# Softmax attention by pairs of heads on the two halves of the array, and one pool of split weights at the low end of the partitions

## Chip, cores and metric

The kernel runs on one core of a Trainium2 chip. The metric is device time in microseconds (us) for one launch: one decoder layer over 512 tokens of width 1024.

## The reference

The layer normalises x, multiplies it by one wide matrix `w_in`, and hands column ranges of the product to three branches: gated linear attention (GLA, 4 heads), softmax attention by blocks (MoBA, 8 heads of 64), and a short convolution. With 512 tokens and blocks of 256 the choice of blocks takes all earlier ones, so that MoBA is plain causal attention with a bias that is linear in the distance:

```
h = rmsnorm(x, g_mix_pre);  gq, gk, gv, gr, glr, mq, mk, mv, sb, sc, sx, glog = split(h @ w_in)
br_a = gla(gq, gk, gv, gr, glr)
br_b = softmax(mq @ mk.T / 8 - slope[head] * distance, causal) @ mv      # 8 heads of 64
br_c = sb * conv3(sc * sx)
merged = sum of sigmoid(glog_i) * (br_i @ w_br_i)
x = x + rmsnorm(merged @ w_out, g_mix_post)
u = conv3(rmsnorm(x, g_ffn_pre) @ ffn_w_up) + b
x = x + rmsnorm((silu(u_gate) * u_up) @ ffn_w_down, g_ffn_post)
```

## The kernel before

**Split weights.** Each large product is made of three matmuls in the type fp32r. `split_w` turns a loaded tile `raw` into `whi` (ACT copies it, line 82) and `wlo` (DVE subtracts, line 83); activations have a high and a low part as well (`hh`/`hl`, `h2h`/`h2l`, `mh`/`ml`, `ahi`/`alo`, and `brA`, `brB`, `brC`). `mm3` (line 91) then issues high by high, high by low and low by high. Where the result has channels on the partitions, `cols_cm` and `up_mm` hold the weights still (the stationary operand, 128 columns) and stream the 512 tokens past them. In `row_major`, which does `w_out` and `w_down`, the activations stand still and 512 columns of weights stream.

**Order of the work.** TensorE's (PE's) instructions stand in the order of the code. A `Stream` called `main` yields after each 12 matmuls of a projection ("a batch" below), and `main.beside(side)` puts pieces of GLA or MoBA between the batches. ACT, DVE and GpSimd (POOL) are ordered by a scheduler; loads are issued on SP's queue.

**MoBA before.** For each of 8 heads `scores` makes two fp32r matmuls for each of the row blocks 3, 2, 1 (line 630 with 128 rows, line 631 with 64 rows) and one fp32 matmul for block 0 (line 633), out of the copies `qs`, `ks`, `kl` that ACT and DVE have made (lines 618 to 622). DVE adds the bias and finds the maximum out of PSUM (line 638), ACT takes the exponential (641), DVE normalises (644). `transposed` turns the probabilities (654), and `mixed` multiplies them by `mv`: 4 fp32 matmuls with 64 stationary columns (669). PSUM has 8 banks: 3 with the tag "main", 5 with "side"; all of MoBA uses the latter.

**Where tiles lie.** Each partition's memory is filled from both ends. Pools without `side` stack up from the low end, pools with `side="right"` from the high end. In the built program, in KB from the start of a partition:

| tile | before | after |
|---|---|---|
| `whi`, `wlo` of the mixer, `w_br`, `w_out` | 190 to 224 | 20 to 62 |
| `whi`, `wlo` of the last `w_out` tile, of `w_up`, `w_down` | 36 to 76 | 20 to 62 |
| `hh`, `hl` | 20 to 52 | 62 to 94 |
| `brA`, `brB`, `brC`, high and low parts | 58 to 130 | 94 to 166 |
| `mh`, `ml` (pool "merged") | 141 to 173 | 175 to 207 |
| `h2h`, `h2l` | 84 to 116 | 98 to 130 |
| `ahi`, `alo` | 130 to 150 | 78 to 98 |

**Buffers of split weights.** In the mixer there are 4 each of `whi` and `wlo` and 2 of `raw`. A second pool "weights2" has 5 and 1; the last tile of `w_out` (k = 7) and the first four of `w_up` (`first_up`, called before the last part of `w_out`) go there. `row_major` keeps its last 4 weight tiles until its last matmul.

Of the kernel before, what the change touches and what calls it, by code (L numbers as in the profile page):

```python
# [17 lines left out]
NT = 4  # L18
# [13 lines left out]
def hybrid_layer(ctx: ExitStack, tc: tile.TileContext, x, g_mix_pre, w_in, gla_w_lr2, gla_b_lr,  # L32
# [34 lines left out]
    def load_w(src, shape):  # L67
        raw = wpool[0].tile([P, wpool[2]], F32, tag="raw", name=nm("raw"), bufs=wpool[1])
# [107 lines left out]
    def load_v(u):  # L176
        raw = wpool[0].tile([P, 2176], F32, tag="raw", name=nm("vraw"), bufs=2)
# [39 lines left out]

    gc = pool("mixer_const")
    b8 = pool("b8")
# [13 lines left out]
    def hi_v(u, half):  # L233
        n = 272 if u == 0 else 256
        hi, lo = [wpool[0].tile([P, wpool[3]], F32R, tag=tag, name=nm(tag), bufs=wpool[4])[:, :4 * n].rearrange(
# [63 lines left out]
    for s in (32, 16, 8, 4, 2, 1):  # L299
# [11 lines left out]
    base = gc.tile([P, T], F32, name="base")  # L311
    nc.gpsimd.iota(base, pattern=[[1, T]], base=-384, channel_multiplier=-1,
                   allow_small_or_imprecise_dtypes=True)
    nc.gpsimd.affine_select(base, base, pattern=[[-1, T]], compare_op=OP.is_ge, fill=-1e37,
                            base=384, channel_multiplier=1)
# [100 lines left out]
    cx = pool("sc", side="right")  # L416
# [62 lines left out]
    def gla_pair(ct, across):  # L479
# [20 lines left out]
        for h in range(2):  # L500
            at.append(gp.tile([P, NT, P], F32, tag="at", name=nm("at"), bufs=3))
# [96 lines left out]
    gp.release()  # L598

    main.beside(iter(["moba"]))
    mp = pool("moba", side="right")
    brB = (bigr("brB_hi"), bigr("brB_lo"))
# [3 lines left out]
    def scores(hd):  # L608
        hs = slice(64 * (hd % 2), 64 * (hd % 2) + 64)
        q, k = mq[hs, hd // 2], mk[hs, hd // 2]  # L610
        bias = mp.tile([P, T], F32, tag="bias", name=nm("bias"), bufs=2)
        nc.gpsimd.tensor_scalar(bias, base, 2.0 ** -(hd + 1), None, op0=OP.mult)

        os_ = slice(64 - hs.start, 128 - hs.start)
        qs = mp.tile([P, T], F32R, tag="qs", name=nm("qs"), bufs=2)
        ks = mp.tile([P, T], F32R, tag="ks", name=nm("ks"), bufs=2)
        kl = mp.tile([P, T], F32R, tag="kl", name=nm("kl"), bufs=2)
# [6 lines left out]
        pr, out_ = {}, {}  # L624
        for i in (3, 2, 1, 0):
            n = (i + 1) * P
            out_[i] = banks[i][:, :n] if i else banks[1][:, 256:384]
            c = slice(i * P, (i + 1) * P)
            if i:
                nc.tensor.matmul(out_[i], qs[:, c], ks[:, :n], start=True, stop=False)  # L630
                nc.tensor.matmul(out_[i], qs[hs, c], kl[hs, :n], start=False, stop=True)  # L631
            else:
                nc.tensor.matmul(out_[i], q[:, c], k[:, :n], start=True, stop=True)
        for i in (3, 2, 1, 0):
            n, ps = (i + 1) * P, out_[i]
            s = mp.tile([P, n], F32, tag=f"p{i}", name=nm("p"), bufs=2)
            mx = sp.tile([P, 1], F32, tag="mx", name=nm("mx"))
            nc.vector.tensor_tensor_reduce(out=s, in0=bias[:, T - n:], in1=ps, scale=-1.0,
                                           scalar=3e38, op0=OP.add, op1=OP.min, accum_out=mx)
            sm = sp.tile([P, 1], F32, tag="sm", name=nm("sm"))  # L640
            last_exp[0] = nc.scalar.activation(s, s, AF.Exp, bias=mx, scale=-1.0, accum_out=sm)
            rc = sp.tile([P, 1], F32, tag="rc", name=nm("rc"))
            nc.vector.reciprocal(rc, sm)
            nc.vector.tensor_scalar(s, s, rc, None, op0=OP.mult)
            pr[i] = s
        return pr

    def transposed(pr):
# [6 lines left out]
        for j in range(3):  # L655
            n = (NT - j) * P if j < 2 else 384
            pt = mp.tile([P, T], F32, tag="pt", name=nm("pt"), bufs=4)
            if j % 2:
                nc.vector.tensor_copy(pt[:, :n], banks[j][:, :n])
            else:  # L660
                nc.scalar.activation(pt[:, :n], banks[j][:, :n], AF.Copy)
            pts.append(pt)
        return pts[0], pts[1][:, :384], pts[2][:, :256], pts[2][:, 256:384]

    def mixed(hd, pts):
        hs = slice(64 * (hd % 2), 64 * (hd % 2) + 64)
# [3 lines left out]
        nc.scalar.activation(brB[0][hs, hd // 2], po[hs], AF.Copy)  # L670
        nc.vector.tensor_tensor(brB[1][hs, hd // 2], po[hs], brB[0][hs, hd // 2].bitcast(F32), OP.subtract)

    def moba():
        pr = pts = None
        for step in range(9):
            nxt = scores(step) if step < 8 else None
            yield 3 if step == 0 else 1
            if pr is not None:
                pts = transposed(pr)
                yield 1  # L680
                mixed(step - 1, pts)
                yield 1
            pr = nxt
# [35 lines left out]
    gc.release()  # L719
# [5 lines left out]
    wpB = pool("weights2")  # L725
# [11 lines left out]
    def row_major(w, kk, resident, getl, epilogue, middle=None):  # L737
# [4 lines left out]
        for k in range(0, kk, 2):  # L742
            raw = load_w(w[k * P:(k + 2) * P].rearrange("(k p) c -> p k c", p=P), (2, D))
            for e in range(2):
                kt = k + e
                wpA = list(wpool)
                if kt == kk - 1:
                    wpool[:] = [wpB, 1, 2048, 1024, 5]
                wts.append([z[:, 0] for z in split_w(raw[:, e:e + 1], 1, D)])
                wpool[:] = wpA  # L750
# [21 lines left out]
    def post_norm(pl, acc, g, res, dst):  # L772
# [4 lines left out]
        def square(n):  # L777
            junk = pl.tile([P, 512], F32, tag="sq", name=nm("sq"), bufs=1)
# [18 lines left out]
    def epi1(t, accs, late=False):  # L797
# [6 lines left out]
        post_norm(ep, accs[t], g2, x1[:, t], x1[:, t])  # L804
# [20 lines left out]
    def first_up():  # L825
        wpA, wpool[:] = list(wpool), [wpB, 1, 2048, 1024, 5]
        ws.extend((part, e, w) for part in range(2) for e, w in enumerate(up_unit(0, part)))
        wpool[:] = wpA
# [4 lines left out]
    wpool[0].release()  # L833
    wpool[:] = [wpB, 1, 2048, 1024, 5]

# [38 lines left out]
    def get_a(k):  # L874
        hi = dn.tile([P, T], F32R, tag="ahi", name=nm("ahi"), bufs=5)
# [40 lines left out]
```

## Time and profile before

| | |
|---|---|
| median of 3 runs | 927.41 us (926.38 to 927.90) |
| the profiled execution | 926.64 us, of which its span 924.8 us |
| PE busy (matmul) | 912.4 us, 99% of the span |
| DVE, ACT, POOL busy | 468.4, 352.2, 76.3 us |
| mean granted clock of PE | 0.994 of full speed |

The span runs from the first to the last instruction; 1.84 us of the execution lie around it. Matmuls overlap one another in the profile (each lasts longer than the time until the next one starts), so what one matmul costs is read from the distance of two starts and not from its length. An fp32 matmul is recorded as two instructions, one in fp32r as one.

### The profile page before, as it was taken

To read this page: it belongs to the slowest core of one execution; us is meant where nothing else is said; L and a number is where in the kernel's file an instruction comes from. 1 tells how busy PE (TensorE), PEld (TensorE's weight loads), DVE (VectorE), ACT (ScalarE), POOL (GpSimd) and SP (SyncE) were. 2 spreads that over 40 slices of the span, in tenths; PEclk is the share of its full clock that TensorE was granted. 3 is DMA by queue.
4 is the path that set the end of the run, shared out by engine and by line. 5 is a ranking of instruction groups with operands and counts; after the bars stand their busy time and mean duration, and the time that the engine had idled before them with its cause. 6 is when DMAs were issued, how large, how long until landed. Compare 5 with 4: busy or idle time off the path is not lost.

```text
span 924.8 us, 11510 instructions
## 1 busy us (share of the span) xinstructions
PE 912.4 (99%) x4723; PEld 737.6 (80%) x4723; DVE 468.4 (51%) x743; ACT 352.2 (38%) x531; POOL 76.3 (8%) x87
## 2 busy tenths in 40 slices
PE   8999989999999999999999999999999999999997
PEld 6988778977667788888888889888888888888885
DVE  5724656487776324242424485665555555433324
ACT  4337644255544323222222354443343333332222
POOL 1001321121010002020201010000000000000000
PEclk8999999999999999999999999999999999999999
DMA  8232312212111132423325511332222333222212
GB/s 255 78 104 73 91 47 57 83 48 90 46 45 47 46 114 68 137 69 105 100 90 184 182 46 69 126 102 92 91 91 91 104 112 103 91 91 91 91 45 92
DMA packets 68616, 85.33 MB, mean 92 GB/s; under 512 B 2693, under 2 KB 62291, under 8 KB 68564
## 3 DMA queue, kind: packets, MB, share of 16 engines
q1 hardware_dynamic: 67522, 84.53, 28.4%
q8 instruction: 37, 0.61, 0.3%
q10 hardware_dynamic: 1042, 0.07, 0.1%
q14 instruction: 15, 0.12, 0.0%
HBM read 82.50 MB, written 2.10 MB: 91 GB/s over the span
## 4 chain that ended last, share of the span: by engine, by line
PE 93%; ACT 4%; DVE 2%; issue 1%; POOL 0%; DVEq 0%; POOLq 0%; ACTq 0%
PE ps L91 84%; PE ps L669 2%; PE ps L563 1%; PE ps L631 1%; PE ps L654 1%; PE ps L169 1%; PE ps L630 1%; ACT whi L82 1%; ACT E L515 1%; PE ps L201 1%; ACT E L516 1%; DVE E L514 1%; DVE wlo L83 0%; PE ps L533 0%; DVE ad L542 0%
## 5 line engine op out<-in xcount | busy, mean ns | idle before, releaser
L83 DVE TENSOR_TENSOR wlo<-raw,whi 128x1024 fp32r<-128x1024 f32 x142 | 177.9, 1255 | 211.7 <-ACT whi L82 211.6
L82 ACT ACTIVATE whi<-raw 128x1024 fp32r<-128x1024 f32 x142 | 149.7, 1058 | 243.6 <-PE ps L91 192.2
L91 PE MATMUL ps<-hh,whi 128*128 128x512 f32 x416 | 168.8, 406 | 0.0
L91 PE MATMUL ps<-hl,whi 128*128 128x512 f32 x416 | 164.5, 395 | 0.0
L91 PE MATMUL ps<-hh,wlo 128*128 128x512 f32 x416 | 164.5, 395 | 0.0
L91 PE MATMUL ps<-h2h,whi 128*128 128x512 f32 (+1 forms) x384 | 142.8, 372 | 0.0
L91 PE MATMUL ps<-h2l,whi 128*128 128x512 f32 (+1 forms) x384 | 142.6, 371 | 0.0
L91 PE MATMUL ps<-h2h,wlo 128*128 128x512 f32 (+1 forms) x384 | 142.6, 371 | 0.0
L91 PEld LDWEIGHTS ps<-hh,whi 128*128 128x128 f32 x416 | 78.2, 188 | 20.4 <-issue 1.7
L91 PEld LDWEIGHTS ps<-hh,wlo 128*128 128x128 f32 x416 | 78.2, 188 | 18.9
L91 PEld LDWEIGHTS ps<-hl,whi 128*128 128x128 f32 x416 | 78.3, 188 | 16.9
L91 PEld LDWEIGHTS ps<-h2l,whi 128*128 128x128 f32 x384 | 72.4, 188 | 12.6
L91 PEld LDWEIGHTS ps<-h2h,whi 128*128 128x128 f32 x384 | 72.3, 188 | 12.5
L91 PEld LDWEIGHTS ps<-h2h,wlo 128*128 128x128 f32 x384 | 72.3, 188 | 12.3
L91 PE MATMUL ps<-whi,ahi 128*128 128x512 f32 x176 | 69.6, 396 | 0.0
L91 PE MATMUL ps<-wlo,ahi 128*128 128x512 f32 x176 | 69.6, 396 | 0.0
L91 PE MATMUL ps<-whi,alo 128*128 128x512 f32 x176 | 69.6, 395 | 0.0
L852 DVE SCALAR_TENSOR_TENSOR u<-ps,cw,u 128x511 f32<-128x511 f32 x44 | 32.9, 747 | 41.7 <-ACT u L849 23.7
L714 POOL TENSOR_TENSOR gate<-gate 128x512 f32<-128x512 f32 x16 | 24.0, 1502 | 217.2 <-DVE gate L712 204.2
L91 PEld LDWEIGHTS ps<-whi,alo 128*128 128x128 f32 x176 | 33.1, 188 | 8.0
L91 PEld LDWEIGHTS ps<-wlo,ahi 128*128 128x128 f32 x176 | 33.1, 188 | 8.0
L91 PEld LDWEIGHTS ps<-whi,ahi 128*128 128x128 f32 x176 | 33.1, 188 | 7.9
(210 smaller groups left out, 1217.8 us busy)
## 6 DMA issues: line engine op xcount, KB each, us to landing
raw<-in_w_in_dram SPq DMA_DIRECT2D x28, 1024.0 KB, 5.5
raw<-in_ffn_w_up_dram SPq DMA_DIRECT2D x22, 1024.0 KB, 5.1
raw<-in_ffn_w_down_dram SPq DMA_DIRECT2D x11, 1024.0 KB, 5.1
x<-in_x_dram SPq DMA_DIRECT2D x8, 512.0 KB, 7.1
raw<-in_w_out_dram SPq DMA_DIRECT2D x4, 1024.0 KB
vraw<-in_w_in_dram SPq DMA_DIRECT2D x4, 512.0 KB, 6.6
raw<-in_w_br_gla_dram SPq DMA_DIRECT2D x4, 512.0 KB, 4.7
raw<-in_w_br_moba_dram SPq DMA_DIRECT2D x4, 512.0 KB, 3.9
```

The source lines that it names most:

```text
L82: nc.scalar.activation(hv, src, AF.Copy)
L83: (sub or nc.vector).tensor_tensor(lv, src, hv.bitcast(F32), op=OP.subtract)
L91: last = nc.tensor.matmul(ps, l, r, start=start and i == 0 and j == 0, stop=stop and i == n - 1 and j == 2)
L169: nc.tensor.transpose(ps[:, i * P:(i + 1) * P], h[:, k * P:(k + 1) * P], ident)
L201: nc.tensor.matmul(ps, warm[:, :P], warm, start=True, stop=True)
L514: nc.vector.tensor_tensor(ev, Lv, Lv[:, :, s - 1:s].to_broadcast([P, nb, 2 * s]), OP.subtract)
L515: nc.scalar.activation(e, e, AF.Abs)
L516: nc.scalar.activation(e, e, AF.Exp, scale=-1.0)
L563: nc.tensor.matmul(po[:, c], l, v[:, j, cv], start=j == 0, stop=j == i)
L669: nc.tensor.matmul(po[hs, j * P:], mv[:, j, hd * 64:(hd + 1) * 64], pts[j], start=j == 0, stop=j == NT - 1)
L714: nc.gpsimd.tensor_tensor(g, g, acc, op=OP.add)
L852: nc.vector.scalar_tensor_tensor(u[:, 1:], ps[:, :T - 1], cw[:, 1, j:j + 1], u[:, 1:], op0=OP.mult, op1=OP.add)
```

## The change

Four things change. (1) One pool of split weights with 5 buffers each of `whi` and `wlo` lies at the low end of the partitions for the whole kernel, the pool of raw tiles (2 buffers) at the high end, and "weights2" is gone; `ahi` and `alo` get a pool at the low end. (2) `scores` and `mixed` work on pairs of heads. The scores are plain fp32 matmuls straight from `mq` and `mk`, one head on rows 0 to 63 of the array and the other on rows 64 to 127, in turns, in two groups (row blocks 3 and 2, then 1 and 0) with a batch between; `mixed` has one head on columns 0 to 63 and the other on 64 to 127, in turns, and leaves PSUM for both heads at once. `qs`, `ks` and `kl` are gone. (3) `base`, from which the biases are made, is computed by POOL when MoBA begins and not in the setup. (4) Smaller: GLA's `at` has 2 buffers and not 3; the squares in the last epilogue are written into `o` and not into a tile of their own.

```
-    wpool = [pool("weights", side="right"), 2, 2176, 1088, 4]
+    wp = pool("weights")
+    rw = pool("raw_weights", bufs=2, side="right")
...
-            hi = wpool[0].tile([P, wpool[3]], F32R, tag="whi", name=nm("whi"), bufs=wpool[4])
-            lo = wpool[0].tile([P, wpool[3]], F32R, tag="wlo", name=nm("wlo"), bufs=wpool[4])
+            hi = wp.tile([P, 1088], F32R, tag="whi", name=nm("whi"), bufs=5)
+            lo = wp.tile([P, 1088], F32R, tag="wlo", name=nm("wlo"), bufs=5)
...
-            at.append(gp.tile([P, NT, P], F32, tag="at", name=nm("at"), bufs=3))
+            at.append(gp.tile([P, NT, P], F32, tag="at", name=nm("at"), bufs=2))
...
+    base = mp.tile([P, T], F32, name="base")
+    nc.gpsimd.iota(base, pattern=[[1, T]], base=-384, channel_multiplier=-1,
+                   allow_small_or_imprecise_dtypes=True)
+    nc.gpsimd.affine_select(base, base, pattern=[[-1, T]], compare_op=OP.is_ge, fill=-1e37,
+                            base=384, channel_multiplier=1)
...
-        nc.scalar.activation(qs[hs], q, AF.Copy)
-        nc.scalar.activation(ks[hs], k, AF.Copy)
-        nc.vector.tensor_tensor(qs[os_, P:], q[:, P:], qs[hs, P:].bitcast(F32), OP.subtract)
-        nc.vector.tensor_copy(ks[os_], ks[hs].bitcast(F32))
-        nc.vector.tensor_tensor(kl[hs], k, ks[hs].bitcast(F32), OP.subtract)
-        banks = {3: psum(), 2: psum(), 1: psum()}
...
-                nc.tensor.matmul(out_[i], qs[:, c], ks[:, :n], start=True, stop=False)
-                nc.tensor.matmul(out_[i], qs[hs, c], kl[hs, :n], start=False, stop=True)
...
+        for group in ((3, 2), (1, 0)):
+            out_ = {}
+            for i in group:
+                for e in range(2):
+                    out_[i, e] = psum() if i else out_[1, e][:, 256:384]
+            for i in group:
+                n = (i + 1) * P
+                for e in range(2):
+                    hs = slice(64 * e, 64 * e + 64)
+                    nc.tensor.matmul(out_[i, e][:, :n], mq[hs, pair, i * P:(i + 1) * P], mk[hs, pair, :n],
+                                     start=True, stop=True)
...
-            nc.tensor.matmul(po[hs, j * P:], mv[:, j, hd * 64:(hd + 1) * 64], pts[j], start=j == 0, stop=j == NT - 1)
+            for e in range(2):
+                hd = 2 * pair + e
+                nc.tensor.matmul(po[64 * e:64 * e + 64, j * P:], mv[:, j, hd * 64:(hd + 1) * 64], pts[e][j],
+                                 start=j == 0, stop=j == NT - 1)
...
+        yield from scores(0)
+        yield 2
+        for pair in range(4):
+            if pair < 3:
+                yield from scores(pair + 1)
+            pts = []
+            for e in range(2):
+                pts.append(transposed(ready[pair][e]))
+                yield 1 + e
+            mixed(pair, pts)
+            yield 1
...
-                wpA = list(wpool)
-                if kt == kk - 1:
-                    wpool[:] = [wpB, 1, 2048, 1024, 5]
...
-        hi = dn.tile([P, T], F32R, tag="ahi", name=nm("ahi"), bufs=5)
-        lo = dn.tile([P, T], F32R, tag="alo", name=nm("alo"), bufs=5)
+        hi = ah.tile([P, T], F32R, tag="ahi", name=nm("ahi"))
+        lo = ah.tile([P, T], F32R, tag="alo", name=nm("alo"))
```

On PE, the scores of the second head before (one head, 7 matmuls in one piece):

```order
L630 MATMUL ps_2083<-ks_2076,qs_2075 128x512
L631 MATMUL ps_2083<-kl_2077,qs_2075 128x512
L630 MATMUL ps_2084<-ks_2076,qs_2075 128x384
L631 MATMUL ps_2084<-kl_2077,qs_2075 128x384
L630 MATMUL ps_2085<-ks_2076,qs_2075 128x256
L631 MATMUL ps_2085<-kl_2077,qs_2075 128x256
L633 MATMUL ps_2085<-mk,mq 128x128
```

And of the second pair of heads now, with the first matmuls of the batch behind them (`hh,whi` and so on are that batch's):

```order
L627 MATMUL ps_2123<-mk,mq 128x512
L627 MATMUL ps_2124<-mk,mq 128x512
L627 MATMUL ps_2125<-mk,mq 128x384
L627 MATMUL ps_2126<-mk,mq 128x384
L93 MATMUL ps_2168<-hh,whi_2164 128x512
L93 MATMUL ps_2168<-hl,whi_2164 128x512
```

The second group of the pair (256, 256, 128 and 128 columns) stands 12 matmuls of the batch later. Two heads have 8 fp32 matmuls where they had 12 in fp32r and 2 in fp32, and neighbours belong to different heads.

The product with `mv` on PE, before (one head) and now (a pair):

```order
L669 MATMUL ps_2174<-pt_2150,mv 64x512
L669 MATMUL ps_2174<-pt_2152,mv 64x384
L669 MATMUL ps_2174<-pt_2154,mv 64x256
L669 MATMUL ps_2174<-pt_2154,mv 64x128
L91 MATMUL ps_2161<-hh,whi_2157 128x512
```

```order
L669 MATMUL ps_2323<-pt_2244,mv 64x512
L669 MATMUL ps_2323<-pt_2283,mv 64x512
L669 MATMUL ps_2323<-pt_2246,mv 64x384
L669 MATMUL ps_2323<-pt_2285,mv 64x384
L669 MATMUL ps_2323<-pt_2248,mv 64x256
L669 MATMUL ps_2323<-pt_2287,mv 64x256
L669 MATMUL ps_2323<-pt_2248,mv 64x128
L669 MATMUL ps_2323<-pt_2287,mv 64x128
```

The same matmuls in the same number; those of two heads now alternate.

On ACT, between the last weights of `w_out` and the first epilogue, before (`raw_4313` and `raw_4323` are of `w_out`, `raw_4333` and `raw_4343` of `w_up`'s first unit, `sq` is the first square of the epilogue of token tile 0):

```order
L82 ACTIVATE whi_4319<-raw_4313 128x1024
L82 ACTIVATE whi_4335<-raw_4333 128x1024
L82 ACTIVATE whi_4339<-raw_4333 128x1024
L82 ACTIVATE whi_4325<-raw_4323 128x1024
L82 ACTIVATE whi_4345<-raw_4343 128x1024
L82 ACTIVATE whi_4349<-raw_4343 128x1024
L779 ACTIVATE sq_4379,ss_730_4377<-ps_4189 128x512
L779 ACTIVATE sq_4383,ss_730_4377<-ps_4190 128x512
```

And now (`raw_4236` and `raw_4246` are of `w_up`'s first unit, `raw_4730` of its second; `sq_4451` and `sq_4455` belong to token tile 3, the last):

```order
L778 ACTIVATE sq_4451,ss_736_4449<-ps_4098 128x512
L175 ACTIVATE h2h<-ps_4423 128x4x128
L161 ACTIVATE h_4404,ss_4403<-x_4072 128x1024
L175 ACTIVATE h2h<-ps_4430 128x4x128
L84 ACTIVATE whi_4242<-raw_4236 128x1024
L84 ACTIVATE whi_4248<-raw_4246 128x1024
L84 ACTIVATE whi_4252<-raw_4246 128x1024
L778 ACTIVATE sq_4455,ss_736_4449<-ps_4099 128x512
L175 ACTIVATE h2h<-ps_4497 128x4x128
L175 ACTIVATE h2h<-ps_4504 128x4x128
L84 ACTIVATE whi_4732<-raw_4730 128x1024
L161 ACTIVATE h_4465,ss_4464<-x_4072 128x1024
```

Three of the four splits for `w_up`'s first unit have moved from ahead of the epilogues into the last one; only one of them (of `raw_4236`) still stands ahead.

## Rows read from the trace of the kernel before

**Rows 1.** The page, busy time of each engine (share) xinstructions.
```profile
PE 912.4 (99%) x4723; PEld 737.6 (80%) x4723; DVE 468.4 (51%) x743; ACT 352.2 (38%) x531; POOL 76.3 (8%) x87
```

**Rows 2.** Waits of PE: engine line <- releaser: us in total, times, longest.
```profile
PE ps L563 <- ACT at L545: 2.5, 2, 2.1
```

**Rows 3.** Chain that ended last, in time order: start us, us, what.
```profile
73.08 1.07 PE ps L433 x4
...
131.01 1.38 PE ps L563 x10
```

**Rows 4.** Line 91 on PE, in a stretch of GLA: busy (x), clock, DMA.
```profile
74.00:131.00 57.00, 44.90 (x180) 1.00 0.25 75
```

**Rows 5.** Timeline of PE in four stages: start us, us, engine, line, operands.
```profile
329.77 0.40 PE L91 MATMUL ps<-hh,wlo 128*128 128x512 f32 x1
...
340.04 0.40 PE L91 MATMUL ps<-brA_lo,whi 128*128 128x512 f32 x1
...
514.85 0.39 PE L91 MATMUL ps<-wlo,mh 128*128 128x512 f32 x1
...
521.88 0.39 PE L91 MATMUL ps<-whi,ml 128*128 128x512 f32 x1
...
649.82 0.39 PE L91 MATMUL ps<-h2l,whi 128*128 128x512 f32 x1
...
659.79 0.39 PE L91 MATMUL ps<-h2h,whi 128*128 128x512 f32 x1
...
804.68 0.39 PE L91 MATMUL ps<-whi,alo 128*128 128x512 f32 x1
...
814.95 0.39 PE L91 MATMUL ps<-wlo,ahi 128*128 128x512 f32 x1
```

**Rows 6.** Timeline of PE, one head of MoBA.
```profile
220.89 0.39 PE L630 MATMUL ps<-ks,qs 128*128 128x512 f32 x1
...
223.23 0.50 PE L91 MATMUL ps<-hh,whi 128*128 128x512 f32 x1
...
230.13 2.37 PE L669 MATMUL ps<-pt,mv 128*64 128x512 f32 x8
232.43 0.50 PE L91 MATMUL ps<-hh,whi 128*128 128x512 f32 x1
```

**Rows 7.** Timeline of PE in GLA: matmuls on halves and quarters of the array.
```profile
141.80 0.38 PE L492 MATMUL ps<-QA,KA 64*128 64x256 f32 x1
141.80 0.37 PE L488 MATMUL ps<-QA,KA 64*128 64x128 f32 x1
...
142.23 0.38 PE L493 MATMUL ps<-QA,KA 64*128 64x128 f32 x2
...
168.31 0.22 PE L533 MATMUL ps<-E 64*64 64x64 f32 x1
...
168.37 0.22 PE L533 MATMUL ps<-E 64*64 64x64 f32 x1
```

**Rows 8.** Windows, the stretch of MoBA: PE, PEld, DVE, ACT, POOL busy (x).
```profile
194.00:317.00 123.00, 123.00 (x530) 86.14 (x529) 83.60 (x207) 61.99 (x130) 13.04 (x8) 1.00 0.18 55
```

**Rows 9.** Groups on POOL in the setup: xcount | busy us, mean ns | idle.
```profile
L314 POOL TENSOR_SCALAR_AFFINE_SELECT base<-base 128x512 f32<-128x512 f32 x1 | 0.6, 607 | 0.0
```

**Rows 10.** Timeline around the end of `w_out`.
```profile
552.72 0.28 PE L91 MATMUL ps<-h2h,whi 128*128 128x256 f32 x1
...
557.48 1.06 ACT L159 ACTIVATE h<-x 128x1024 f32<-128x1024 f32 x1 [0.16 <-DVE x L791]
...
559.48 1.29 DVE L161 SCALAR_TENSOR_TENSOR h<-x,rs,g 128x1024 f32<-128x1024 f32 x1 [0.66 <-POOL rs L138]
...
562.22 1.04 PE L169 MATMUL ps<-ident,h 128*128 128x128 f32 x8
```

**Rows 11.** Groups on DVE: xcount | busy us, mean ns | idle, releaser.
```profile
L83 DVE TENSOR_TENSOR wlo<-raw,whi 128x1024 fp32r<-128x1024 f32 x142 | 177.9, 1255 | 211.7 <-ACT whi L82 211.6
```

**Rows 12.** DMA issues: xcount, KB each, median us from issue to landing.
```profile
raw<-in_ffn_w_up_dram SPq DMA_DIRECT2D x22, 1024.0 KB, 5.1
```

More of the change, by code (lines that the diff above doesn't have):

```diff
@@ L67, in load_w @@
     def load_w(src, shape):
-        raw = wpool[0].tile([P, wpool[2]], F32, tag="raw", name=nm("raw"), bufs=wpool[1])
+        raw = rw.tile([P, 2176], F32, tag="raw", name=nm("raw"))
         n = 1
@@ L176, in load_v @@
     def load_v(u):
-        raw = wpool[0].tile([P, 2176], F32, tag="raw", name=nm("vraw"), bufs=2)
+        raw = rw.tile([P, 2176], F32, tag="raw", name=nm("vraw"))
         n = 272 if u == 0 else 256
@@ new lines, in scores @@
+    def scores(pair):
+        bias, pr = [], [{}, {}]
+        for e in range(2):
+            bias.append(mp.tile([P, T], F32, tag="bias", name=nm("bias"), bufs=2))
+            nc.gpsimd.tensor_scalar(bias[e], base, 2.0 ** -(2 * pair + e + 1), None, op0=OP.mult)
+        for group in ((3, 2), (1, 0)):
[9 more added lines that the diff above has]
+                                     start=True, stop=True)
+            for i in group:
+                n = (i + 1) * P
+                for e in range(2):
+                    ps = out_[i, e][:, :n]
+                    s = mp.tile([P, n], F32, tag=f"p{i}", name=nm("p"), bufs=4)
+                    mx = sp.tile([P, 1], F32, tag="mx", name=nm("mx"))
+                    nc.vector.tensor_tensor_reduce(out=s, in0=bias[e][:, T - n:], in1=ps, scale=-1.0,
+                                                   scalar=3e38, op0=OP.add, op1=OP.min, accum_out=mx)
+                    sm = sp.tile([P, 1], F32, tag="sm", name=nm("sm"))
+                    last_exp[0] = nc.scalar.activation(s, s, AF.Exp, bias=mx, scale=-1.0, accum_out=sm)
+                    rc = sp.tile([P, 1], F32, tag="rc", name=nm("rc"))
+                    nc.vector.reciprocal(rc, sm)
+                    nc.vector.tensor_scalar(s, s, rc, None, op0=OP.mult)
+                    pr[e][i] = s
+            yield 1
+        ready.append(pr)
@@ L656, in transposed, with mixed @@
             n = (NT - j) * P if j < 2 else 384
-            pt = mp.tile([P, T], F32, tag="pt", name=nm("pt"), bufs=4)
+            pt = mp.tile([P, n], F32, tag=f"pt{j}", name=nm("pt"), bufs=2)
             if j % 2:
-                nc.vector.tensor_copy(pt[:, :n], banks[j][:, :n])
+                nc.vector.tensor_copy(pt, banks[j][:, :n])
             else:
-                nc.scalar.activation(pt[:, :n], banks[j][:, :n], AF.Copy)
+                nc.scalar.activation(pt, banks[j][:, :n], AF.Copy)
             pts.append(pt)
-        return pts[0], pts[1][:, :384], pts[2][:, :256], pts[2][:, 256:384]
-    def mixed(hd, pts):
-        hs = slice(64 * (hd % 2), 64 * (hd % 2) + 64)
+        return pts[0], pts[1], pts[2][:, :256], pts[2][:, 256:384]
+    def mixed(pair, pts):
         po = psum()
         for j in range(NT):
-            nc.tensor.matmul(po[hs, j * P:], mv[:, j, hd * 64:(hd + 1) * 64], pts[j], start=j == 0, stop=j == NT - 1)
-        nc.scalar.activation(brB[0][hs, hd // 2], po[hs], AF.Copy)
-        nc.vector.tensor_tensor(brB[1][hs, hd // 2], po[hs], brB[0][hs, hd // 2].bitcast(F32), OP.subtract)
-    def moba():
[L674 to L683, printed above, removed]
+            for e in range(2):
+                hd = 2 * pair + e
+                nc.tensor.matmul(po[64 * e:64 * e + 64, j * P:], mv[:, j, hd * 64:(hd + 1) * 64], pts[e][j],
+                                 start=j == 0, stop=j == NT - 1)
+        nc.scalar.activation(brB[0][:, pair], po, AF.Copy)
+        nc.vector.tensor_tensor(brB[1][:, pair], po, brB[0][:, pair].bitcast(F32), OP.subtract)
+    ready = []
+    def moba():
+        yield from scores(0)
[4 more added lines that the diff above has]
+            pts = []
+            for e in range(2):
+                pts.append(transposed(ready[pair][e]))
+                yield 1 + e
+            mixed(pair, pts)
+            yield 1
     main.beside(moba())
@@ L777, in square @@
         def square(n):
-            junk = pl.tile([P, 512], F32, tag="sq", name=nm("sq"), bufs=1)
+            junk = pl.tile([P, 512], F32, tag="sq", name=nm("sq"), bufs=1) if dst is res else dst[:, ns[n]]
             nc.scalar.activation(junk, acc[n], AF.Square, accum_out=ss[:, n:n + 1])
```

55 lines of the change are left out of this document (8 added, 47 removed).

## The prediction

> **What bounds the kernel now.** I read the page's busy times first: PE is busy for 99% of the span and no other engine for more than 51% [rows 1]. The waits come next. PE's longest by line are 2.5 us in GLA [rows 2], so a change pays where it takes time off PE's instructions. Then the chain that ended last, to see where PE is not what counts. From 73.08 us (line 433) to 131.01 us (line 563) it runs through ACT and DVE, and PE's part in that stretch waits at its end for `at` [rows 2, 3]. Inside it stand 180 projection matmuls [rows 4], and what they gain I count as nothing. Elsewhere the chain is PE's.
>
> Last comes the timeline of PE, from start to start, at four places [rows 5]. The rows are the same kind of work, fp32r with 128 stationary and 512 streamed columns, but the distance has two values:
>
> - gates and `w_br`: 329.77 to 340.04, 44 steps, 233.4 ns (weights at 190 to 224 KB, the other operand below 130);
> - `w_out`: 514.85 to 521.88, 31 steps, 226.8 ns (both above 140 KB);
> - `w_up`: 649.82 to 659.79, 44 steps, 226.6 ns (both below 116 KB);
> - `w_down`: 804.68 to 814.95, 44 steps, 233.4 ns (weights below 76 KB, `ahi` above 130).
>
> What sorts these four is whether the two operands lie at the same end. Neither end is slow by itself: high with high and low with low both give 226.7. Which of the two is stationary doesn't matter either. The border lies about 128 to 130 KB, since `brC_hi` (up to 130) counts as low and `ahi` (from 130) as high. I take 6.7 ns a matmul for "opposite" against "same".
>
> **Placement, term by term.** Counts are from the loops, places from the table.
>
> - `cols_cm`: 52 column tiles of 24 matmuls, 1,248, from opposite to same. Without the 180 that are hidden, 1,068 x 6.7 ns = 7.2 us gained (8.4 if none is hidden).
> - `w_down`: 22 x 8 x 3 = 528, from opposite to same (`ahi` now 78 to 98): 3.5 us gained.
> - `w_out`: 192, of which 168 (all but k = 7) had both operands high. Now `mh` is high and the weights low: 168 x 6.7 = 1.1 us lost.
> - `w_br`: 288. The branch tiles now straddle the border: `brA_lo`, `brB_lo` and the first tile of `brA_hi` lie below it, the rest above. That is 10 of 36 matmuls to the same end, 0.5 us gained (bounds 0 and 1.9).
> - `w_up`: only the last of the 8 tiles of `h2l` goes above 128 KB, one matmul in 24: 0.3 us lost.
>
> Sum: 9.8 us gained.
>
> A page of the Trainium skill speaks against this term. "SBUF — State Buffer", section "Who interferes with whom", gives PE two independent read ports, one for streamed and one for stationary operands, and says that PE never waits for anyone. By it no place of a tile would change a matmul, and the term would be nothing. The spacings above differ by 3% between stages that differ in nothing else that I can see, so I follow them.
>
> **MoBA on PE.** One head's product with `mv` (1,280 fp32 columns in 8 instructions) takes PE from 230.13 to 232.43, 2.30 us. One head's scores take it from 220.89 to 223.23, 2.34 us [rows 6]. Now a head's scores are fp32 with the same 1,280 columns, so I price them too at 2.30. For a pair:
>
> - before: 2 x 2.34 + 2 x 2.30 = 9.28 us;
> - halves wholly in turn: 4 x 2.30 = 9.20 us, nothing gained;
> - halves wholly side by side: 2 x 2.30 = 4.60 us, 4.68 us gained.
>
> Do halves run side by side? Where GLA has one head on rows 0 to 63 and the next on 64 to 127, line 492 of the first and line 488 of the second start at the same 141.80, though line 493 of the first, which starts at 142.23, is earlier in the program [rows 7]. On quarters of the array, lines 533 and 534 take all four quarters in turn, and a quarter's next matmul starts 60 ns later [rows 7]; that covers columns too. So I expect overlap, not turns. It need not be whole: if starts kept the program's order, each group would end later by about one instruction of its widest matmul, which is 2.30 / 2 x 512 / 1,280 = 0.46 us for the group of 512, 0.23 for that of 256 and 0.46 for `mixed`, 1.15 a pair. The gain is then 4 x 3.53 = 14.1 us instead of 4 x 4.68 = 18.7. I take the middle, 16.4.
>
> On this the skill is strict. "TensorE: Matmul & The Clock Gate", section "The mechanism" of Part 3, has matmuls start and end strictly in program order. By that rule the 14.1 would hold; the start of line 488 ahead of line 493 speaks against it, so I don't go to that end.
>
> The transposes stay as they are. ACT and DVE lose the making of `qs`, `ks`, `kl` and half the evacuations of `mixed`. DVE was busy for 83.6 of 123 us there [rows 8]; the stretch shrinks by about 18 us, and even with nothing taken from DVE it would be busy 83.6 of 105. So PE should remain the bound, but tighter: a group of scores takes 4 of the 5 side banks, and the next group needs one of them read by DVE within a batch of 12 (2.8 us). I allow 1.5 us for such stalls in all (0 to 5).
>
> **Edits at nothing.** `base` costs POOL two operations of 0.6 us [rows 9] at the start of MoBA, ahead of the first bias; four batches (11 us) stand between the first scores and the first transposes and cover it. If the cover failed, it would cost 1 to 3 us once. `at` with 2 buffers makes POOL's clearing for the second pair wait for the last line 563 of the first, a whole step of GLA before its use. A second `raw` in the FFN helps a load that PE wasn't waiting for. The squares in `o` wait for the output DMA of two token tiles earlier.
>
> **The end of `w_out`, a new wait.** The four resident tiles of `w_out` hold four of the five buffers, so three splits of `w_up`'s first unit can begin only during its last 12 matmuls. Those splits themselves come in time: PE needs the second one a whole `up_mm` after 552.72. But they stand ahead of the last square on ACT and of the epilogue on DVE, and the split of the following unit stands ahead of `h` for token tile 3 (last order rows). Its `raw` buffer comes free only with those splits, about 1.5 us after 552.72 (two subtractions of 1.26 [rows 11] after buffers that free 1.4 us before it). Add the load, 5.1 us [rows 12], a pass of ACT, 1.06, and the way from line 159's start to line 161's end, 557.48 to 560.77, 3.3 us [rows 10]: 11.0 us. PE asks for it at 562.22, 9.5 us after 552.72 [rows 10]; before it had 1.45 us to spare. So PE waits about 1.5 us, and with the DVE work that is moved ahead I take 2.0 (bounds 0 and 4).
>
> **Sum.** 926.64 (the profiled execution) - 9.8 - 16.4 + 1.5 + 2.0 = 903.9. That execution lies 0.8 us below the median of the runs shown, so I forecast 904.7.
>
> **Rivals.**
>
> - *The halves take turns.* For it: two heads share one PSUM bank in `mixed`, which no row here shows with 128 rows. Against it: [rows 7]. Then MoBA gains 0.3 us and has no stall: 926.64 - 9.8 - 0.3 + 2.0 + 0.8 = 919.3.
> - *Placement does nothing* (what the page on the State Buffer would have), the spacing being due to something else that sorts the four stages alike. For it: four stages are few. Then 904.7 + 9.8 = 914.5. With the first rival together: 929.1.
> - *Each change of half empties the array.* This ends slower. The old scores change between 128 and 64 rows at nearly each matmul: 2,304 fp32r columns at 233.4 ns for 512 would be 1.05 us, the fp32 piece 0.23, and 2.34 was taken [rows 5, 6]; the 1.06 us left over 6 changes are 0.18 a change. A pair now has 16 matmuls in turns; 16 x 0.18 x 4 = 11.5 us on top of the first rival's 919.3 is 930.8. It decides from 0.16 us a change on. Against it: starts 60 ns apart in [rows 7].
> - *Stalls in MoBA.* If DVE reads each group of scores too late for the next, PE waits a few us a pair: 8 to 16 us over the stage, 911 to 919.
>
> **How the numbers follow.** My forecast: 0.65. With all its bounds at one end (overlap 18.7 or 14.1, stalls 0 or 5, wait 0 or 4, `w_br` 1.9 or 0, GLA's 180 gained or not) it would be 896 or 913; since they won't all fall alike, its own range is 899 to 911. Placement nothing: 0.12. Turns: 0.09. Stalls: 0.07. Turns and no placement: 0.03; emptying: 0.03; left over 0.01. The range of 898 to 916 holds the first, the second and about half of the stalls, 0.8. A measurement of this kernel tells 0.2% (1.9 us) from no change. Faster by more than that: 0.65 + 0.12 + 0.09 + 0.07 = 0.93; slower 0.03 + 0.03 = 0.06; the same 0.01.
>
> **What would show it.** Spacing from start to start in gates and `w_down` 226.7 (placement right) or 233.4 (wrong); in `w_out` 233.4; in `w_br` a mixture. In MoBA, line 627 with starts of both halves inside one another, 2.3 to 3.0 us of PE a pair, and line 669 the same. PE waiting for DVE's line 163 at about the first `w_up`, 0 to 4 us. Wrong would be: line 627 or 669 at 4.6 us a pair, waits for PSUM in MoBA above 5 us, or a span of GLA that grows because a fifth buffer lets splits in ahead of its chain.

## The result, and the profile after

The changed kernel takes 904.06 us (median of 4 runs, 903.63 to 905.66) against 927.28 (926.38 to 927.90) before: ratio 0.9753, 95% interval 0.9737 to 0.9770. The forecast was 904.7. The profiled execution is the longest of the four, 905.66 us with a span of 903.6. Line numbers have shifted: line 91 (a projection matmul) is now 93, line 563 (GLA's product with `at`) is 559, and lines 161 and 169 (DVE's normalised tokens `h`, and PE's transposes of them) are 163 and 171.

Page of after, busy times, which answers to [rows 1] (PEld is PE's loading of stationary operands):

```profile
PE 886.8 (98%) x4723; PEld 731.7 (81%) x4723; DVE 453.8 (50%) x715; ACT 337.8 (37%) x511; POOL 74.8 (8%) x87
```

PE has lost 25.6 us of work, more than the span has lost (21.2). So it waits more than before. Waits of PE after, as in [rows 2] (us in total, times, longest):

```profile
PE ps L171 <- DVE h L163: 5.2, 3, 2.4
PE ps L559 <- ACT at L541: 3.0, 2, 2.7
...
PE ps L93 <- ACT hh L175: 0.9, 1, 0.9
```

Spacing from start to start after, as in [rows 5] (timeline of PE; two rows each from gates to the end of `w_br`'s first column tile, of `w_out`, of `w_down`):

```profile
316.53 0.39 PE L93 MATMUL ps<-hh,whi 128*128 128x512 f32 x1
...
329.22 0.39 PE L93 MATMUL ps<-brC_hi,wlo 128*128 128x512 f32 x1
...
498.26 0.39 PE L93 MATMUL ps<-whi,ml 128*128 128x512 f32 x1
...
508.52 0.39 PE L93 MATMUL ps<-wlo,mh 128*128 128x512 f32 x1
...
800.38 0.39 PE L93 MATMUL ps<-whi,alo 128*128 128x512 f32 x1
...
810.35 0.39 PE L93 MATMUL ps<-wlo,ahi 128*128 128x512 f32 x1
```

56, 44 and 44 steps: 226.6, 233.2 and 226.6 ns. Gates and `w_down` have become fast and `w_out` slow, as forecast. But all of `w_br` is fast, where a mixture was forecast: the first two rows span all 36 matmuls of a column tile of `w_br`, and 26 of these, `brC_hi` among them, lie above the border and against weights at 20 to 62 KB are "opposite" by the prediction's rule.

One pair of heads after, from PE's chain (start, us, what), which answers to [rows 6]:

```profile
211.49 1.70 PE ps L627 x8
...
216.14 0.85 PE ps L627 x8
...
230.41 2.31 PE ps L669 x16
...
296.75 224.31 PE ps L93 x984
```

A pair takes 1.70 + 0.85 + 2.31 = 4.86 us where two heads took 9.28, and none of PE's waits lies in MoBA. The last row is the run of projections from the end of MoBA to `w_out`.

The end of `w_out` after, from the chain that ended last, beside [rows 10]:

```profile
533.41 5.16 DMA raw<-in_ffn_w_up_dram
...
538.60 1.07 ACT whi L84
...
539.69 1.22 DVE wlo L85
...
541.64 1.29 DVE h L163
...
543.07 1.10 PE ps L171 x8
```

This is the new wait that the prediction worked out, through the load that it named. The timeline gives 2.36 us of PE's idle time for it (in brackets):

```profile
543.07 1.10 PE L171 MATMUL ps<-ident,h 128*128 128x128 f32 x8 [2.36 <-DVE h L163]
```

Two costs stand in no term of the prediction. The first is on the chain at the start:

```profile
22.53 1.22 DVE wlo L85
...
24.47 1.29 DVE h L163
...
42.45 0.46 PE ps L326 x5
```

The fifth buffer lets the first split of the columns in ahead of `h` for the last token tile on DVE. The stage ends at 42.45 us; the same transposes began at 41.20 before.

The second is PE's clock. Windows of after (stretch, its us, busy PE, PEld, DVE, ACT, POOL, granted clock, DMA share, GB/s):

```profile
129.00:131.00 2.00, 0.35 (x2) 0.30 (x2) 1.63 (x4) 1.21 (x3) 0.95 (x1) 0.99 0.00 0
131.00:134.00 3.00, 2.67 (x13) 2.49 (x12) 1.43 (x2) 1.78 (x4) 0.00 (x0) 0.50 0.02 5
...
541.00:543.00 2.00, 0.00 (x0) 0.00 (x0) 1.28 (x1) 0.00 (x0) 0.55 (x1) 1.00 0.00 1
...
545.00:547.00 2.00, 2.00 (x12) 2.00 (x11) 0.65 (x2) 0.00 (x0) 0.00 (x0) 0.50 0.00 0
```

After each of the two long waits PE was granted 0.50, the lower of its two levels (1.2 GHz), for some 3 us. In GLA, line 559 then takes 2.50 us for the 10 instructions that took 1.38 before [rows 3].

### The profile page after: what moved, and what is told of

It is laid out like the page before. It is cut to its first block, busy times and chain, and to the rows that moved or that the text cites. A ratio compares the mean times of both kernels' runs of the same rounds, so it can differ in the third digit from the quotient of the medians.

```text
span 903.6 us, 11488 instructions
## 1 busy us (share of the span) xinstructions
PE 886.8 (98%) x4723; PEld 731.7 (81%) x4723; DVE 453.8 (50%) x715; ACT 337.8 (37%) x511; POOL 74.8 (8%) x87
## 4 chain that ended last, share of the span: by engine, by line
PE 89%; ACT 4%; DVE 3%; DMA 1%; issue 1%; POOL 0%; ACTq 0%; DVEq 0%; POOLq 0%
PE ps L93 83%; PE ps L627 1%; PE ps L559 1%; PE ps L669 1%; PE ps L652 1%; DMA vraw<-in_w_in_dram 1%; ACT whi L84 1%; DVE wlo L85 1%; ACT E L511 1%; DMA raw<-in_ffn_w_up_dram 1%; ACT E L512 1%; PE ps L171 1%; DVE E L510 1%; PE ps L529 0%; DVE ad L538 0%
## 5 line engine op out<-in xcount | busy, mean ns | idle before, releaser
L93 PE MATMUL ps<-hh,whi 128*128 128x512 f32 x416 | 166.6, 401 | 0.0
L93 PE MATMUL ps<-hh,wlo 128*128 128x512 f32 x416 | 162.3, 390 | 0.0
L93 PE MATMUL ps<-hl,whi 128*128 128x512 f32 x416 | 162.2, 390 | 0.0
L873 DVE TENSOR_TENSOR alo<-a,ahi 128x512 fp32r<-128x512 f32 x22 | 15.2, 692 | 55.9 <-ACT ahi L872 55.9
L872 ACT ACTIVATE ahi<-a 128x512 fp32r<-128x512 f32 x22 | 13.9, 632 | 75.4 <-PE ps L93 65.4
L93 PE MATMUL ps<-whi,hh 128*128 128x256 f32 (+1 forms) x128 | 38.7, 302 | 0.9 <-ACT hh L175 0.9
```

Source lines behind the costliest of these rows:

```text
L93: last = nc.tensor.matmul(ps, l, r, start=start and i == 0 and j == 0, stop=stop and i == n - 1 and j == 2)
L872: nc.scalar.activation(hi, a[:, k], AF.Copy)
L873: nc.vector.tensor_tensor(lo, a[:, k], hi.bitcast(F32), OP.subtract)
```

## The experiments

Given for each run are the median of 4 or 5 executions, in brackets the shortest and the longest, and the ratio to the kernel before with its 95% interval; the two runs of matmuls alone (eight places, first bytes) are one execution each. Each run has its own runs of the kernel before on the same chip. The runs on pairs, places, turns and splits shared one chip (before: 926.24 us), those on eight places, the repeat, the batch and everything moved a second (926.87), and the last four a third (926.45).

**Pairs alone.** The kernel before with the hunks of the change in `scores`, `transposed`, `mixed` and `moba`, nothing else; one line of them:

```
-    def scores(hd):
+    def scores(pair):
```

> The kernel before with the pairs of heads in MoBA alone; weights, pools and splits lie where they lay. The prediction's terms for the pairs (16.4 gained, 1.5 of stalls) give 927.3 - 14.9 = 912.4 us. The trace after the change, read as two heads wholly side by side (4.86 us a pair instead of 9.28, no stall), gives 927.3 - 17.7 = 909.6. Rival: what looks like the pairs' gain belongs partly to where the weights lie (fewer us in the batches between), and then the pairs alone give less: 915 or more. If halves took turns: 927.

909.73 us (908.43 to 910.17), ratio 0.9817 (0.9802 to 0.9832). That is 16.5 us: the 17.7 of the trace lie in the interval and the prediction's 14.9 just outside it. PE's chain of this run has the pairs as they are in the changed kernel (lines 624 and 666 are 627 and 669 there):

```profile
210.69 1.70 PE ps L624 x8
...
215.39 0.85 PE ps L624 x8
...
229.83 2.30 PE ps L666 x16
```

The gain belongs to the pairs, wherever the weights lie.

**Places alone.** The changed kernel with the same hunks taken back (so the fifth buffer, `base` and `at` are still as changed):

```
-    def scores(pair):
+    def scores(hd):
```

> The changed kernel with MoBA head by head as before: the places of the tiles and the one pool alone. The prediction's terms (9.8 gained, 2.0 for the wait at the end of w_out) give 927.3 - 7.8 = 919.5 us. The traces, read stage by stage, give the changed kernel's 904.1 + 17.7 = 921.8, since the start has grown by 1.2 and part of the gain in batches of 12 is lost. Rival, places change nothing: 927.3 + 2.4 + 1.2 = 930.9. If the sum of this run's gain and that of the pairs alone is far from 23.2, the two parts hang together.

921.96 us (920.53 to 923.16), ratio 0.9951 (0.9934 to 0.9968), as read. The two parts gain 16.5 and 4.3, together 20.8, while both at once gain 23.1 (the repeat below). The intervals of the three together, some 2.5 us, don't tell this difference from nothing. In both of these profiles the clock falls to 0.50 behind GLA's wait and a batch of 12 there takes 4.18 and 4.31 us (2.80 before); a loss of about 1.4 us that each part pays by itself, and both at once pay once, would fit more than half of it.

**Heads in turn.**

```
-            for i in group:
-                n = (i + 1) * P
-                for e in range(2):
+            for e in range(2):
+                for i in group:
+                    n = (i + 1) * P
...
-        for j in range(NT):
-            for e in range(2):
+        for e in range(2):
+            for j in range(NT):
```

> The changed kernel with the same matmuls in MoBA, but those of one head of a pair all ahead of the other's, in each group of scores and in the product with mv. Theory: heads overlap only where neighbours in the program belong to different halves; then a pair takes about 1.7 + 0.85 us more for scores (less what the last of one head and the first of the other overlap) and 2.3 - 0.5 for the product with mv, some 4 us a pair, and the time is 904.1 + 14 to 17 = 918 to 921. Rival 1: the gain comes from leaving out fp32r and its changes of shape, and the order of the heads does nothing: 904. Rival 2: PE looks far ahead and runs the other half whenever it is free: 904 to 907.

910.68 us (909.03 to 911.47), ratio 0.9833 (0.9815 to 0.9850): between the theories. PE's chain of this run:

```profile
210.17 1.71 PE ps L627 x8
...
214.82 0.86 PE ps L627 x8
...
229.10 2.30 PE ps L669 x8
231.50 1.46 PE ps L669 x6
```

The scores cost what they cost in turns of one: two matmuls of one head stand ahead of the other head's, and they still overlap wholly. In the product with `mv`, four stand ahead, and 1.46 us of the second head are left over; with the 0.10 between the rows, 1.56 x 4 = 6.2 us, most of the 7 to 8 us that are lost (0.9833 against 0.9748 to 0.9753). So PE runs the other half past a few earlier instructions, not past any number: order matters only from there on. How many it passes can be counted from the starts in the trace, where each fp32 matmul is two instructions. In the product the second head's first (230.59) starts together with the first head's fifth (230.58), ahead of the sixth to eighth (230.80 to 231.13): past three. In the scores, on rows and not on columns, it starts with the first of four (210.11 and 210.10), also past three. In GLA before, line 488 of the second head (141.80) starts ahead of the second instruction of line 492 and both of line 493: three again. That PE never passes more is not shown. Leaving out fp32r is not the cause of the gain: by the rows of [rows 6] (2.34 us for a head's scores in fp32r, 2.30 for the same number of fp32 columns) it is worth some 0.08 us a pair, an estimate.

**Two splits held back.** The first split of the columns and the first of `w_up`'s second unit, behind the last activations of `transposed_split` on ACT and DVE (an order on each engine, no wait between engines).

```
+            if behind:
+                after(ia, last_split[0][0], "not ahead of the activations")
+                after(iv, last_split[0][1], "not ahead of the activations")
...
+                hi, lo = split_w(raw[:, :, e * P:(e + 1) * P], kk, P, behind=c0 == C_GR and u + e == 0)
...
+        return [split_w(raw[:, :, e * P:(e + 1) * P], KD, P, behind=jp == 1 and part + e == 0) for e in range(2)]
```

> The changed kernel with two splits held back on ACT and DVE: the first of the columns of w_in after v, and the first of w_up's second unit, each put behind the last activations of its stage (transposed_split of token tile 3) and no longer ahead of them. Theory: the wait of 2.36 us for h (line 163) at the end of w_out comes from the second, and 1.2 us of the start stage from the first; without both, 904.1 - 2.4 - 1.2 = 900.5 us, PE's wait for line 163 falls from 5.2 us to about 2.2, and the v stage ends near 41.2 instead of 42.45. Rival: the three splits of w_up's first unit ahead of the last square hold h back as well, so that about 1 us of the wait stays: 901.5. Rival: the split of the second unit now comes late for its own matmuls, and the wait moves there: 903 or more.

903.08 us (902.16 to 903.25), ratio 0.9746 (0.9731 to 0.9760): no difference from the changed kernel that can be told. The start did what was expected (chain of this run):

```profile
41.07 0.46 PE ps L332 x5
```

1.38 us earlier, and the first `at` products of GLA begin 1.40 earlier too. Then most of it is lost again (windows of this run):

```profile
128.00:130.00 2.00, 0.76 (x2) 0.50 (x2) 1.23 (x3) 1.60 (x4) 0.54 (x1) 0.69 0.00 0
130.00:132.00 2.00, 1.93 (x10) 1.89 (x10) 0.83 (x1) 1.39 (x3) 0.00 (x0) 0.50 0.03 8
132.00:134.00 2.00, 2.00 (x7) 1.71 (x7) 1.35 (x5) 0.39 (x1) 0.36 (x1) 0.50 0.17 33
134.00:136.00 2.00, 2.00 (x7) 1.52 (x7) 0.85 (x2) 0.00 (x0) 1.00 (x2) 0.60 1.01 341
```

The clock is low for nearly 7 us, and the next batch takes 4.20 us, not 2.97. At the end of `w_out` the first rival holds, by more than it said (timeline of this run):

```profile
542.18 1.07 PE L176 MATMUL ps<-ident,h 128*128 128x128 f32 x8 [1.65 <-DVE h L168]
```

1.65 us of the 2.36 stay, since three splits of `w_up`'s first unit still stand ahead of the last epilogue on DVE.

**Eight places.** Edit: the matmuls are all there is, on tiles `pa` to `ph` of 640 columns.

```
+    for st in PLACES:
+        for mv in PLACES:
...
+                    nc.tensor.matmul(ps, tiles[st][:, 512:640], tiles[mv][:, :512], start=i == 0, stop=i == 11)
```

> A kernel that leaves out the whole computation and writes zeros: fp32r matmuls with 128 stationary and 512 streamed columns, 36 for each ordered pair of eight places at 20, 60, 90, 110, 123, 130, 150 and 190 KB of a partition (pa to ph), spacing from start to start. The prediction's rule (opposite ends of a border between 123 and 130 KB are slow, whichever operand is stationary): 233.4 ns for the 30 pairs that straddle the border, 226.7 for the 34 others. Second theory, from w_br after the change: slow only with the stationary operand above the border and the streamed one below it, 15 pairs; stationary low and streamed high gives 226.7. Third theory: no place matters, and the spacing in the kernel comes from what else uses the memory in those stages: all 64 alike.

All pairs take 226.7 ns from start to start (the first, which opens the kernel, apart). Groups on PE by line (streamed, stationary; count, busy us, mean ns):

```profile
L56 PE MATMUL ps<-pa,ph 128*128 128x512 f32 x36 | 8.3, 389 | 0.0
L56 PE MATMUL ps<-ph,pa 128*128 128x512 f32 x36 | 8.3, 389 | 0.0
L56 PE MATMUL ps<-pe,pf 128*128 128x512 f32 x36 | 8.3, 389 | 0.0
```

The ends do nothing. The rule of the prediction and the second theory both fall. What the kernels have and this run doesn't was found in the first bytes of the tiles in the built programs: those from the low end begin at 160 modulo 256, those from the high end at 224, in both kernels. Here all began at 0. That would also explain why all of `w_br` became fast: its tiles and the weights now both come from the low end.

**The changed kernel again.**

> The changed kernel itself once more, beside the next two on the same chip: 903 to 905 us. If the low clock that its profile shows from 131 to 134.6 us (0.50, line 559 in 2.50 us instead of 1.38) belongs to the kernel, it is there again; if it comes and goes from one execution to the next, it may be missing, and the span is then 1.1 us shorter.

903.73 us (902.13 to 904.89), ratio 0.9748 (0.9734 to 0.9763). The clock falls in GLA again (4.24 us for a batch), but not at the end of `w_out`, where it did the first time, though PE waits there nearly as long (2.19 us). The two profiled spans are 903.6 and 901.9.

**One batch more in GLA.**

```
-            yield 1
+            yield 2 if s == 0 and ct == 0 else 1
```

> The changed kernel with one batch of 12 matmuls more ahead of GLA's first line 559 (a batch that otherwise stands later), so that PE no longer waits 3.0 us there for at. Theory: the wait goes (2.7 us) and with it the fall of the clock to 0.50 that follows it (1.1 us in the changed kernel's profile, 1.5 to 2.6 in others): 904 - 3 to 5 = 899 to 901, granted clock 1.00 from 125 to 140 us. Rival: GLA's chain on ACT and DVE bounds the stretch, and the batch taken out of a later step makes PE wait there (the second pair's steps): 903 to 904.

900.57 us (899.78 to 901.56), ratio 0.9718 (0.9704 to 0.9731): the theory. PE waits 0.4 us in that place (3.0 before the edit), and the granted clock is 1.00 throughout 125 to 140 us. The wait at the end of `w_out` is still there (2.28 us), and in this profile the clock fell to 0.50 behind it.

**Everything moved.** The splits held back, the batch, and two of the three splits behind the last epilogue's work.

```
+            ws.extend((1, e, split_w(raw1[0][:, :, e * P:(e + 1) * P], KD, P, behind=norm_ins[0] if e else done))
+                      for e in range(2))
```

> The kernel with the two splits held back (as in that run) and the batch more in GLA, and of the three splits of w_up's first unit that stand ahead of the last epilogue on ACT and DVE two moved behind it: the third tile's split to stand behind the last square on ACT and the last x on DVE, the fourth's behind h of token tile 3. Theory: the 2.2 us left of PE's wait for h at the end of w_out go too, so 1.4 (start) + 2.7 to 5 (GLA) + 2.2 to 2.4 = 6.3 to 8.8 below the changed kernel: 895 to 898 us. Rival: the third tile's split now comes late for its own matmuls, and some 1 to 2 us of the wait move there: 897 to 900.

896.22 us (895.64 to 896.43), ratio 0.9669 (0.9656 to 0.9683). The end of `w_out` in the chain of this run (window 524 to 545 us, so the first and the last row are parts), PE alone:

```profile
523.80 5.21 PE ps L97 x34
529.00 0.87 PE ps L175 x8
529.88 5.75 PE ps L97 x48
535.63 0.87 PE ps L175 x8
536.50 8.52 PE ps L97 x71
```

No wait is left there, and none has come in its place. (What was left of it was 1.65 us. The 2.2 of the expectation are PE's wait for `h` at the start, which the kernel before has too.)

**First bytes.** Again matmuls alone, with other places.

```
-PLACES = {"pa": 20, "pb": 60, "pc": 90, "pd": 110, "pe": 123, "pf": 130, "pg": 150, "ph": 190}
+PLACES = {f"r{32 * i}": (20 + 16 * i) * 1024 + 32 * i for i in range(8)}
```

> Again a kernel that leaves out the whole computation and writes zeros. In the run on eight places all tiles began at a multiple of 512 bytes, and all 64 pairs cost 226.7 ns. In the kernels the tiles of pools from the low end begin at 32 bytes modulo 128, those from the high end at 96, so that opposite ends also means a difference of 64 bytes modulo 128. Here eight tiles begin at 0, 32, 64, ... 224 bytes modulo 256 (r0 to r224), 24 matmuls for each ordered pair, with 512 columns, and for r0 and r32 as the stationary one also with 256. Theory: what counts is the difference of the two operands' first bytes; pairs that differ by 64 (modulo 128) take 233.4 ns, pairs with equal remainder 226.7; pairs that differ by 32 or 96 have no row yet and may go either way. Rival: the first bytes don't matter either, all alike at 226.7; then the spacing in the kernel is due to what ACT, DVE and DMA do beside PE.

The theory, in a sharper form. Timeline of PE for r96 as the stationary operand: 22 steps of the pair with r96 itself (first two rows), then 22 of the pair with r128 (last two):

```profile
155.40 0.40 PE L57 MATMUL ps<-r 128*128 128x512 f32 x1
...
160.40 0.62 PE L57 MATMUL ps<-r 128*128 128x512 f32 x2
160.85 0.40 PE L57 MATMUL ps<-r,r 128*128 128x512 f32 x1
...
165.99 0.87 PE L57 MATMUL ps<-r,r 128*128 128x512 f32 x3
```

227.3 and 233.6 ns. Over all pairs, from the starts in the trace: equal bytes modulo 256 settle at 226.7 (after one to five matmuls at 228 to 236), the streamed operand 64 bytes further gives 229, every other difference 232 to 234, one of 128 too. So the remainder counts modulo 256, not 128 as I had it. That a whole 256 makes no difference is shown by the changed kernel: its weight buffers lie 4,352 bytes (17 x 256) apart, and gates and `w_br` are fast with all of them. The kernels' 160 and 224 differ by 64 in the slow direction (the stationary operand 64 further).

**The kernel before, 64 bytes.** A tile of 64 bytes as the first at the high end, so that all pools begin at 160 modulo 256.

```
+    pad = pool("pad", side="right")
+    pad.tile([P, 16], F32, name="pad")
```

> The kernel before with nothing but a tile of 64 bytes put at the high end, so that every pool from the high end moves down by 64 bytes and begins at 32 modulo 128 like those from the low end. No tile changes its end. Theory of the first bytes: gates, w_br, w_down and all of w_out at 226.7 ns. By stages: 1,068 x 6.7 = 7.2 (less what batches lose), w_down 3.5, w_br 288 x 6.7 = 1.9, together 11 to 12.6 below before: 926.7 - 11.5 = 915. Rival, the prediction's (which end counts): no change, 926.7.

916.92 us (916.50 to 917.47), ratio 0.9897 (0.9883 to 0.9910). No tile changed its end. Timeline of PE, 44 steps from gates into `w_br`, 226.6 ns (233.4 in [rows 5]):

```profile
329.25 0.39 PE L93 MATMUL ps<-hl,whi 128*128 128x512 f32 x1
...
339.22 0.39 PE L93 MATMUL ps<-brA_hi,whi 128*128 128x512 f32 x1
```

And the long run of PE from the end of MoBA to `w_out`, first in the chain of before:

```profile
316.67 226.18 PE ps L91 x972
```

and in that of this run:

```profile
316.72 220.55 PE ps L93 x972
```

5.6 us there and 3.5 in `w_up` and `w_down` (355.23 to 351.71 by the same view). In this profile the clock is at 0.50 again behind GLA's wait, which takes back 2.6 (line 565, as 563 was, in 2.50 us, and a batch in 4.19).

**The changed kernel, 64 bytes.** The same tile.

> The changed kernel with the same 64 bytes at the high end: mh and ml, which come from the high end, then begin at 32 modulo 128 like the weights. Theory of the first bytes: w_out from 233.4 to 226.7 ns, 192 x 6.7 = 1.3 us less, 904 - 1.3 = 902.5. Rival, which end counts: w_out stays at 233.4, 904.

902.26 us (900.92 to 905.48), ratio 0.9740 (0.9720 to 0.9760): too wide to tell 1.3 us by itself, but the spacing does. `w_out` in the timeline of this run, 44 steps, 226.6 ns:

```profile
498.35 0.39 PE L95 MATMUL ps<-wlo,mh 128*128 128x512 f32 x1
...
508.32 0.39 PE L95 MATMUL ps<-whi,mh 128*128 128x512 f32 x1
```

**Everything moved, 64 bytes.**

> The version with the splits moved and the batch more in GLA (896.2 us) and the 64 bytes at the high end: 896.2 - 1.3 = 894.9 us by the theory of the first bytes, 896.2 if it is the end that counts.

894.23 us (894.22 to 894.69), ratio 0.9653 (0.9639 to 0.9666): the best version, about 9 us below the changed kernel (0.9653 against 0.9748 to 0.9753). The step from everything moved is 1.5 us by the ratios (1.3 expected); the two intervals touch.

## Why the prediction was right, step by step

The stages of the two profiled spans, 924.8 and 903.6, add up as follows (starts of the same work in the two traces):

| step | predicted, us | measured, us |
|---|---|---|
| matmuls at 226.7 and 233.4 ns (long run -4.6, batches in MoBA -1.3, `w_down` -3.5 as in the kernel before with 64 bytes) | -9.8 | -9.4 |
| pairs of heads, 4 x (9.28 - 4.86) | -16.4, stalls +1.5 | -17.7, no stall |
| end of `w_out`: wait 2.36, slower matmuls, then 1.5 at the low clock in `w_up` | +2.0 | +4.2 |
| start: a split ahead of `h` | 0 | +1.3 |
| GLA from 42 us to the first scores, low clock included | 0 | +0.6 |
| sum | -22.7 | -21.0 |

The long run is 972 matmuls in 226.18 us before and 984 in 224.31 after; the 12 more cost 2.75, so 4.6 are gained. From the first scores to that run it was 120.91 us and is 99.17 with 12 matmuls fewer: 19.0 gained, of which 17.7 are the pairs'. The 0.2 that are missing to 21.2 lie in rounding and in the last epilogue.

That the forecast of 904.7 came within 0.7 us of 904.06 is in part luck: by the table the pairs gave 2.8 us more than was forecast for them (1.3 of overlap, 1.5 of stalls that did not come), while the end of `w_out`, the start, GLA and the matmuls' spacing cost 4.5 more, and the profiled execution, which the table follows, lies 1.6 us above the median.

- **Placement.** The size was right and the step that gave it was wrong: "What sorts these four is whether the two operands lie at the same end", with a border at 128 to 130 KB. The ends only decided the first bytes, and the four stages couldn't tell one from the other; `w_br` after the change, eight places, and 64 bytes in the kernel before do. The term's own misses follow from it: `w_br` gains its upper bound of 1.9 and not 0.5, `w_up` loses nothing by it. The batches of 12 gain less (2.94 to 2.97 us against 2.99 to 3.00), which fits that an equal pair needs some matmuls to settle in the run on first bytes. The rule of the Trainium skill, "SBUF — State Buffer", section "Who interferes with whom", that PE has two independent read ports and never waits on anyone, agrees with the run on eight places (226.7 throughout). The section is about other engines; if it is taken to hold between PE's own two reads, as the prediction took it, the run on first bytes speaks against it, where PE alone goes at 233.
- **MoBA.** Right, with the size at its upper end (17.7 of 18.7). The halves run wholly side by side: 2.31 us for a pair's product, 2.30 for one head's before [rows 6]. The middle that was taken between overlap and program order was too low by 1.3, and the 1.5 of stalls did not come. The rule of the Trainium skill, "TensorE: Matmul & The Clock Gate", section "The mechanism" of Part 3, that matmuls start and end in program order, would have asked for 1.15 us a pair more, 5.75 with the 4.60 of whole overlap. The 4.86 leave no room for it, and heads in turn show how far PE goes past that order.
- **The new wait.** Right in place, chain and size (2.36 for 2.0). Missing was what comes after it: the clock, 1.5 us in that execution and nothing in the repeat's.
- **Edits at nothing.** `base`, `at` and the second `raw` cost nothing that shows. The fifth buffer did, in the v stage: "a fifth buffer lets splits in ahead of its chain" was named among what would be wrong, but for GLA, and had no price.

What stays open: whether the kernel before ever loses its clock in GLA (its one profile shows 1.00 there, behind a wait of 2.1; its other runs go from a mean clock of 0.996 and a span of 923.1 to 923.4 us to 0.993 and 925.6 to 926.3, but not where); what decides whether the clock falls behind a wait; and why the remainder modulo 256 matters to PE at all.

## What to carry to other kernels

Where like matmuls differ by 3%, look at the first bytes of both operands modulo 256 before moving anything: 64 bytes of padding were worth about 1% here. Independent heads on halves of the array took about half their time here as long as not more than two fp32 matmuls of one stood ahead of the other's; with four, part of it was lost, and three were not run. A saved microsecond ahead of a wait comes back only if the wait goes too: fill it with work that is due anyway, and see what a further buffer lets in ahead of the work that PE waits for.

## What the hardware showed that was not expected

- fp32r matmuls, 128 stationary and 512 streamed columns: 226.7 ns with equal first bytes modulo 256, 229 with the streamed operand 64 further, 232 to 234 otherwise. With 256 streamed columns equal bytes are no longer the fastest: 119.3 and 119.7 ns for them, 113.7 to 119.6 for the others, with two stationary tiles (run on first bytes).
- PE runs instructions of the other half of the array ahead of earlier ones, up to three in every place counted (an fp32 matmul is two): with two matmuls ahead nothing is lost, with four 1.56 of 2.30 us are. It did so on halves by rows and by columns.
- The granted clock fell to 0.50 for 3 to 7 us, in or just behind PE waits of 2.2 to 2.8 us: in seven of the nine profiles that have the long wait in GLA, and in three of the seven that have the one at the end of `w_out` (1.65 to 2.36 us). The length of the wait alone doesn't decide it: behind 2.69 us in GLA (heads in turn) and 2.30 at the end of `w_out` the clock stayed at 1.00. A fall cost 1.3 to 2.6 us. With the waits gone (everything moved) it stayed at 1.00 there, and the four runs lie within 0.8 us.
